# One tile for the split weights, at two offsets: an encoder trunk on one Trainium2 core

## The chip, the core and the metric

The kernel runs on one core of one Trainium2 chip. The metric is the device time of one execution in microseconds; the time of a kernel is the median over its runs. The granted TensorE clock of the profiled execution is 0.999 of full speed.

## What is computed

Two layers of a streaming encoder on 512 tokens of width 1024, all in float32. Cut to what matters here:

```python
def swiglu(x, w_gate, w_up, w_down):
    return (silu(x @ w_gate) * (x @ w_up)) @ w_down        # 1024 -> 2816 -> 1024

for l in range(2):
    x = x + 0.5 * swiglu(rms_norm(x, ffn1_norm[l]), ...)
    h = rms_norm(x, mix_norm[l])
    p = h @ w_in[l]                                        # 1024 -> 1696
    attn = mla_group(...)                                  # latent attention, 8 heads
    conv = conv_group(...)                                 # GLU, causal depthwise conv, LayerNorm
    x = x + concat(attn, conv) @ w_out[l]
    x = x + 0.5 * swiglu(rms_norm(x, ffn2_norm[l]), ...)
    x = rms_norm(x, post_norm[l])
```

The four feed-forward networks (two a layer) hold most of the arithmetic.

## The kernel before

**Products in three parts.** A float32 operand is split into a high part, rounded to the reduced format fp32r that TensorE takes, and a low part, the rest. A product is three matmuls, `mm3` (L171 to L175): high weights with high data (L172), high weights with low data (L173), low weights with high data (L174). In most places the weights are the stationary operand, which a LDWEIGHTS brings into the array ahead of its matmul, and the data are the moving one. Each matmul is 128 by 128 by 256 or 512 columns. In the latent products of the mixer (`latent_k`, `queries`, `keys`, `up_kv`) it is the other way round: data stationary, weights moving.

**Where weights come from.** `load_w` (L149) loads a block of 1024 columns into a tile raw by SyncE's DMA queue, ScalarE casts it to a tile wh (L153), and VectorE (for one kind GpSimd) subtracts to get the tile wl (L159). `half_w` does the same for the first blocks (L1114 to L1118). These are the plain products: the first chunk of each feed-forward network, the down projection of its last chunk, and all of the mixer's products with weights.

**The chunks of the feed-forward network.** `ffn_body` goes through eleven pairs of 256 hidden columns in four chunks. The first chunk of two pairs is computed plainly. The later pairs go through `pair` (L418) with a scheme of seven products in place of eight, on halves of 256 tokens: sums and differences of weight blocks and of activation halves are made by VectorE, and the products are of 256 columns. `product` (L374) takes three matmuls for each; `product_joined` (L385) has high and low data of 256 columns beside each other in one tile xj and needs two: L391 with 512 columns (high weights with both), L392 with 256 (low weights with the high data). Its callers make the weights in two ways. `split_into` (L259) casts a quarter tile fr or raw to wh (L262) and subtracts to wl (L264). `summed` (L411) casts to wh (L415), and its low part is a tile ls, made from the negated copy (L407) to which GpSimd's DMA queue adds the block from memory (L408). `down` (L479) does the same for the down projection of the two middle chunks with 256-column matmuls; its data are ring tiles.

**Where data lie.** Normalized data, products of the gate and most sums are ring tiles r (2048 bytes for each partition, 35 of them). `operands` (L324) makes the sums of the data: those named in `JOINED` and in halves as xj (`joined`, L326), the others in ring tiles (`halved`, L332), and one kind, b22 of the second half, in two tiles xs.

**Where the tiles begin.** Tiles lie in the pools in the order in which their tags first come up. Small tiles `gap0` (16 floats) and `gap1` (32 floats) stand between raw, wh and wl (L1110), and `gap` (`GAP`, L117) stands in the pool of small tiles. Counted modulo 256 bytes with a ring tile as 0, the tiles begin at: wh +64, wl +192; all tiles of the feed-forward pool (fr, xj, xs, ls and others) +96. Every block of 128 columns within a weights tile is 512 bytes, and half a ring tile is 1024, so these offsets hold for every matmul.

**What sets the order.** The tile framework places each engine's instructions by a planned timeline; `tc.issue_after` pins some behind others. A cast waits until the last matmul that reads its slot is done. wh and wl have four slots each.

Of the kernel before, what the change touches and what calls it, by code (L numbers as in the profile page):

```python
# [7 lines left out]
FP = mybir.dt.float32  # L8
FR = mybir.dt.float32r
# [3 lines left out]
ALU = mybir.AluOpType  # L13
AX = mybir.AxisListType

P = 128
D = 1024
S = 512
# [13 lines left out]
NF = F // P  # L32
EPS = 1e-6
WC = 1024
GAP = 96
HS = S // 2
RING = 35
WIDE = 6
# [11 lines left out]
POOLW = "wo"  # L50
# [29 lines left out]
def encoder_kernel(ctx: ExitStack, tc: tile.TileContext, xT, consts, vecs, rgain, wgu1, wd1, wdq1,  # L80
# [6 lines left out]
    wpool = ctx.enter_context(tc.tile_pool(name="w", bufs=4))  # L87
# [4 lines left out]
    def nm(s):  # L92
        uid[0] += 1
        return f"{s}{uid[0]}"
# [21 lines left out]

    small.tile([P, GAP], FP, tag="gap", name="gap", bufs=1)  # L117
    V, A, G, T = nc.vector, nc.scalar, nc.gpsimd, nc.tensor
# [30 lines left out]
    def load_w(src, w, kind=""):  # L149
        raw = wpool.tile([P, WC], FP, tag="raw", name=nm("raw"), bufs=3)  # L150
        nc.sync.dma_start(out=raw[:, :w], in_=src)
        hi = wpool.tile([P, WC], FR, tag="wh", name=nm("wh"))
        order["cast"] = A.copy(hi[:, :w], raw[:, :w]).ins  # L153
        lo = low()
        if kind == "sum":
            A.activation(lo[:, :w], raw[:, :w], AF.Copy, scale=-1.0)
            G.dma_start(out=lo[:, :w], in_=src, accum_op=ALU.add)
            return hi, lo
        (G if kind in POOLW.split() else V).tensor_tensor(lo[:, :w], raw[:, :w], hi[:, :w].bitcast(FP),  # L159
                                                          ALU.subtract)  # L160
        return hi, lo

    def low():
        return wpool.tile([P, WC], FR, tag="wl", name=nm("wl"))

    order = {}

# [82 lines left out]
    def groups(srcs, rhs, ws=None):  # L250

        ws = ws or [load_w(src, WC) for src in srcs]
        os = [bank() for _ in srcs]
        for ks in (range(KD - 1), range(KD - 1, KD)):
            for o, w in zip(os, ws):
                group(o, w, rhs, ks, KD)
        return os

    def split_into(q, src, w=WC):  # L259

        hi = wpool.tile([P, WC], FR, tag="wh", name=nm("wh"))
        A.copy(hi[:, :w], src[:, :w])  # L262
        lo = low()
        order["lo"] = V.tensor_tensor(lo[:, :w], src[:, :w], hi[:, :w].bitcast(FP), ALU.subtract).ins  # L264
        return hi, lo

    def ffn(l, gx, norm, wgu, wd, wdq, gain, done, w0=None, halved=KD):
# [3 lines left out]
    def ffn_body(fpool, l, gx, norm, wgu, wd, wdq, gain, done, w0, halved):  # L271
# [2 lines left out]

        def quarter():
            return fpool.tile([P, WC], FP, tag="fr", name=nm("fr"), bufs=4)
# [124 lines left out]
        def subtracted(w, src, n=WC):  # L404

            lo = fpool.tile([P, WC], FR, tag="ls", name=nm("ls"), bufs=2)
            A.activation(lo[:, :n], src[:, :n], AF.Copy, scale=-1.0)  # L407
            G.dma_start(out=lo[:, :n], in_=w, accum_op=ALU.add)  # L408
            return lo

        def summed(w, src, n=WC, lo=None):  # L411

            lo = subtracted(w, src, n) if lo is None else lo
            hi = wpool.tile([P, WC], FR, tag="wh", name=nm("wh"))
            A.copy(hi[:, :n], src[:, :n])  # L415
            return hi, lo

        def pair(p, quartered):  # L418

            a11, a12, a21, a22, s3 = quarters(wgu[l, p], WC, p == CHUNKS[0][1])  # L420
            bx, by, bz = bank(), (bank(), bank()), (bank(), bank())
            product(bx, split_into("a11", a11), "b11", True, True)
            a = copied(tmp(), bx)
            product_joined(by, summed(wgu[l, p, 1], a12), "b21", True)
# [6 lines left out]
            for c, main, rest in parts(by):  # L431
                V.tensor_tensor(a[:, c], a[:, c], main, ALU.add)
                V.tensor_tensor(a[:, c], a[:, c], rest, ALU.add)
                if c.start == 0:
                    A.activation(s[:, 0:HS], a[:, 0:HS], AF.Silu)
            V.tensor_tensor(s[:, 0:HS], s[:, 0:HS], a[:, HS:S], ALU.mult)
            product(bx, split_into("s2", a11), "t2", False, True)
            r2 = wide(fpool.tile([P, WC], FP, tag="e", name=nm("e"), bufs=1))
            copied(r2[:, 0], bx)
            product_joined(bz, split_into("s3", s3), "t3", True)  # L440
            d = [copied(tmp(), o) for o in bz]
            for t in d:
# [97 lines left out]
        for p0, p1 in CHUNKS:  # L540
# [54 lines left out]
            for m in range(halved if last else KD):  # L595
                if m in ahead:
                    pd, w = ahead[m]
# [440 lines left out]
    class Finish:  # L1038
# [37 lines left out]
        def part(self, h, src, first):  # L1076
            for t in range(2):
                i = T.matmul(self.ss[:, 2 * h + t:2 * h + t + 1], src[:, t * P:(t + 1) * P], ones[:, 0:1],
                             start=first and h == 0 and t == 0, stop=not first, skip_group_check=True)
            return i.ins  # L1080
# [26 lines left out]
    st = Stats()  # L1107
    f = gained(0, "g1", gx, first_gain)
    f(0)
    w0 = [tuple(wpool.tile([P, w], t, tag=tag, name=nm(tag), bufs=n) for t, tag, n, w in (  # L1110
        (FP, "raw", 3, WC), (FP, "gap0", 1, 16), (FR, "wh", 4, WC), (FP, "gap1", 1, 32), (FR, "wl", 4, WC)))[::2]
        for _ in range(2)]

    def half_w(q, gu):  # L1114
        raw, hi, lo = (v[:, gu * 512:(gu + 1) * 512] for v in w0[q])
        nc.sync.dma_start(out=raw, in_=wgu1[0, 0, q, :, gu * 512:(gu + 1) * 512])
        A.copy(hi, raw)  # L1117
        V.tensor_tensor(lo, raw, hi.bitcast(FP), ALU.subtract)  # L1118
    for m in KS:
        if m:  # L1120
            nc.sync.dma_start(out=x[:, m, :], in_=xT[m])
# [6 lines left out]
    w0 = [w[1:] for w in w0]  # L1128
# [172 lines left out]
```

## Time and profile before

| | us |
|---|---|
| median of 3 runs | 1783.02 (1781.78 to 1783.49) |
| the profiled execution | 1781.53 |
| its span, first to last instruction | 1779.8 |
| TensorE, matmuls | 1768.6 busy, 11430 instructions |
| VectorE | 1486.0 busy |
| ScalarE | 1094.9 busy |
| GpSimd | 383.3 busy |

Matmuls are pipelined: the duration of one runs past the start of the next, so busy time and mean duration say little about what a matmul costs. The distance between the starts of neighbouring matmuls does, and the timeline shows it. A group's row has line, engine, operation, output and inputs with buffer numbers left out, shape, count, then busy time, mean duration of one in ns, and the idle time of the engine before it with what ended it.

### The profile page before, as it was taken

What the parts mean: (1) busy time and instruction counts of PE and PEld (TensorE: products, weight loads), DVE (VectorE), ACT (ScalarE), POOL (GpSimd) and SP (SyncE); (2) the same over time, 40 slices, a digit from 0 to 9 for tenths busy, and PEclk for the clock granted to TensorE, in tenths of its full rate; (3) what the DMA queues carried; (4) which work ended last, traced back from release to release, by engine and by line L of the source; (5) the groups of instructions that cost most, each with busy time, mean ns of one, the idle gap of its engine ahead of it and who ended that gap; (6) DMA issues with size and microseconds to landing.
All of it is one profiled execution on the core that took longest, in us unless ns stands there. A gap on an engine that the chain in (4) does not pass through costs nothing.

```text
span 1779.8 us, 29441 instructions
## 1 busy us (share of the span) xinstructions
PE 1768.6 (99%) x11430; PEld 1558.0 (88%) x11430; DVE 1486.0 (83%) x2309; ACT 1094.9 (62%) x1699; POOL 383.3 (22%) x315
## 2 busy tenths in 40 slices
PE   9999999999999999999999999999999999999998
PEld 7899999888678899999888999998976788999997
DVE  7998988588965989998779989876989559999883
ACT  5576766456953575757645757554768435757664
POOL 1000000247822000000310000002576410000002
PEclk9999999999999999999999999999999999999999
DMA  5657574324203466665426575743260125575742
GB/s 170 165 140 186 136 189 114 109 86 124 71 25 101 124 162 162 159 166 131 123 66 167 125 197 124 198 112 112 80 157 24 58 68 155 150 180 140 186 117 74
DMA packets 71947, 228.28 MB, mean 128 GB/s; under 512 B 8448, under 2 KB 9600, under 8 KB 71808
## 3 DMA queue, kind: packets, MB, share of 16 engines
q1 hardware_dynamic: 55536, 171.87, 30.5%
q0 software_dynamic: 16128, 54.53, 18.3%
q8 instruction: 89, 1.46, 0.3%
q14 instruction: 50, 0.41, 0.1%
q10 hardware_dynamic: 144, 0.00, 0.0%
HBM read 222.19 MB, written 2.10 MB: 126 GB/s over the span
## 4 chain that ended last, share of the span: by engine, by line
PE 91%; DVE 5%; ACT 2%; issue 1%; DMA 1%; SPq 0%; ACTq 0%; DVEq 0%
PE ps L172 24%; PE ps L174 24%; PE ps L173 23%; PE ps L391 11%; PE ps L392 6%; DVE cv L972 1%; PE ps L921 1%; DVE mx L880 1%; PE ps L899 1%; DVE wl L264 1%; PE ps L876 0%; PE ps L678 0%; PE ps L216 0%; PE ps L914 0%; DVE r L902 0%
## 5 line engine op out<-in xcount | busy, mean ns | idle before, releaser
L172 PE MATMUL ps<-r,wh 128*128 128x256 f32 (+1 forms) x2556 | 808.8, 320 | 1.7 <-ACT wh L1117 0.6
L173 PE MATMUL ps<-r,wh 128*128 128x256 f32 (+1 forms) x2556 | 807.4, 316 | 0.8 <-DVE r L180 0.4
L174 PE MATMUL ps<-r,wl 128*128 128x256 f32 (+1 forms) x2364 | 753.9, 321 | 0.0
L172 PEld LDWEIGHTS ps<-r,wh 128*128 128x128 f32 x2556 | 480.6, 188 | 51.0 <-issue 3.7
L173 PEld LDWEIGHTS ps<-r,wh 128*128 128x128 f32 x2556 | 480.1, 188 | 42.7 <-DVE r L180 2.5
L174 PEld LDWEIGHTS ps<-r,wl 128*128 128x128 f32 x2364 | 444.1, 188 | 38.5 <-DVE wl L159 0.7
L391 PE MATMUL ps<-xj,wh 128*128 128x512 f32 x864 | 302.5, 390 | 0.0
L153 ACT CAST wh<-raw 128x1024 fp32r<-128x1024 f32 (+3 forms) x148 | 132.4, 900 | 227.9 <-PE ps L173 140.3
L262 ACT CAST wh<-fr 128x1024 fp32r<-128x1024 f32 (+1 forms) x160 | 157.8, 986 | 103.5 <-DVE fr L428 53.2
L159 DVE TENSOR_TENSOR wl<-raw,wh 128x1024 fp32r<-128x1024 f32 (+3 forms) x132 | 142.6, 1089 | 92.5 <-ACT wh L153 91.7
L408 POOL DMA_DIRECT2D ls<-in_wgu x72 | 62.5, 868 | 724.3 <-ACT ls L407 522.5
L264 DVE TENSOR_TENSOR wl<-fr,wh 128x1024 fp32r<-128x1024 f32 (+1 forms) x160 | 182.8, 1143 | 20.2 <-ACT wh L262 20.2
L391 PEld LDWEIGHTS ps<-xj,wh 128*128 128x128 f32 x864 | 160.8, 188 | 29.1
L392 PE MATMUL ps<-xj,ls 128*128 128x256 f32 x576 | 161.3, 280 | 0.0
L978 POOL TENSOR_TENSOR y<-y,pr 128x495 f32<-128x495 f32 (+29 forms) x90 | 120.3, 1339 | 46.6 <-ACT pr L976 41.2
L262 ACT CAST wh<-raw 128x1024 fp32r<-128x1024 f32 (+1 forms) x100 | 97.9, 979 | 42.1 <-PE ps L173 21.1
L264 DVE TENSOR_TENSOR wl<-raw,wh 128x1024 fp32r<-128x1024 f32 (+1 forms) x100 | 113.8, 1138 | 11.8 <-ACT wh L262 11.2
L392 PEld LDWEIGHTS ps<-xj,ls 128*128 128x128 f32 x576 | 108.1, 188 | 0.0
L209 POOL TENSOR_TENSOR r<-r,t 128x512 f32<-128x512 f32 x45 | 75.3, 1681 | 133.3 <-ACT t L205 132.7
L407 ACT ACTIVATE ls<-fr 128x1024 fp32r<-128x1024 f32 (+1 forms) x56 | 56.1, 1001 | 73.3 <-PE ps L392 41.5
L972 DVE SCALAR_TENSOR_TENSOR cv<-m,vec,cv 128x511 f32<-128x511 f32 (+14 forms) x120 | 88.1, 734 | 4.6 <-ACT cv L968 3.0
L408 POOL DMA_DIRECT2D ls<-in_wdq x32 | 27.6, 863 | 258.6 <-ACT ls L407 258.6
(258 smaller groups left out, 2921.5 us busy)
## 6 DMA issues: line engine op xcount, KB each, us to landing
fr<-in_wgu SPq DMA_DIRECT2D x112, 512.0 KB, 4.2
ls<-in_wgu POOLq DMA_DIRECT2D x72, 512.0 KB, 6.6
raw<-in_wgu SPq DMA_DIRECT2D x62, 512.0 KB, 4.6
fr<-in_wdq SPq DMA_DIRECT2D x48, 384.0 KB, 4.7
ls<-in_wdq POOLq DMA_DIRECT2D x32, 384.0 KB, 4.9
raw<-in_wd SPq DMA_DIRECT2D x32, 384.0 KB, 3.2
raw<-in_wd SPq DMA_DIRECT2D x32, 256.0 KB, 2.8
raw<-in_wcv SPq DMA_DIRECT2D x16, 512.0 KB, 3.6
```

Of the source, the lines that this page charges most:

```text
L153: order["cast"] = A.copy(hi[:, :w], raw[:, :w]).ins
L159: (G if kind in POOLW.split() else V).tensor_tensor(lo[:, :w], raw[:, :w], hi[:, :w].bitcast(FP), ALU.subtract)
L172: T.matmul(o, lh, rh, start=first, stop=False, skip_group_check=free)
L173: T.matmul(o, lh, rl, start=False, stop=False, skip_group_check=free)
L174: order["mm"] = T.matmul(o, ll, rh, start=False, stop=last, skip_group_check=free).ins
L262: A.copy(hi[:, :w], src[:, :w])
L264: order["lo"] = V.tensor_tensor(lo[:, :w], src[:, :w], hi[:, :w].bitcast(FP), ALU.subtract).ins
L391: T.matmul(o, w[0][:, c], both, start=start and k == 0, stop=False, skip_group_check=True)
L392: last = T.matmul(o[:, 0:HS], w[1][:, c], both[:, 0:HS], start=False, stop=k == 3, skip_group_check=True).ins
L408: G.dma_start(out=lo[:, :n], in_=w, accum_op=ALU.add)
L972: V.scalar_tensor_tensor(acc[:, s:], u[c][:, :S - s], tap(k), acc[:, s:], ALU.mult, ALU.add)
L978: order["conv"] = G.tensor_tensor(ys[c][:, s:], ys[c][:, s:], pr[:, s:], ALU.add).ins
```

## The change

Three things are changed.

*One weights tile.* wh, wl, gap0 and gap1 are gone. A tile `weights` of 2 x 4 x 1024 floats and 48 more holds four slots for the high parts and then four for the low ones. `part(j, moved)` hands out the next slot of the high (0) or low (1) parts. For `load_w` and `half_w` a slot begins at 0 from a ring tile (modulo 256 bytes); for `split_into` and `summed` (`moved`) it begins 16 floats further for a high part and 48 for a low one: +64 and +192, as before. A moved slot reaches into the first bytes of the slot behind it; where the kind changes from moved to plain, one slot is skipped.

*Order.* `in_turn` pins the high casts behind each other in the order of the program, and the low subtractions of each engine too.

*The pool of the feed-forward network.* Its tags are brought up at the start in another order, xj, xs, a gap of 48 floats, ls, and then the rest, and `GAP` is 72. So xj and xs begin at 0 from a ring tile, ls and fr at +192.

The diff, cut to its core:

```diff
-GAP = 96
+GAP = 72
+WN = 4
+WOFF = 16, 48
@@ load_w
-        hi = wpool.tile([P, WC], FR, tag="wh", name=nm("wh"))
-        order["cast"] = A.copy(hi[:, :w], raw[:, :w]).ins
+        hi = part(0)
+        order["cast"] = in_turn("h", lambda: A.copy(hi[:, :w], raw[:, :w]))
         lo = low()
...
-        (G if kind in POOLW.split() else V).tensor_tensor(lo[:, :w], raw[:, :w], hi[:, :w].bitcast(FP),
-                                                          ALU.subtract)
+        e = G if kind in POOLW.split() else V
+        in_turn(e, lambda: e.tensor_tensor(lo[:, :w], raw[:, :w], hi[:, :w].bitcast(FP), ALU.subtract))
         return hi, lo

-    def low():
-        return wpool.tile([P, WC], FR, tag="wl", name=nm("wl"))
+    weights = wpool.tile([P, 2 * WN * WC + WOFF[1]], FR, name="weights", bufs=1)
+    used, was = [0, 0], [False, False]
+
+    def part(j, moved=False):
+        if was[j] and not moved:
+            used[j] += 1
+        was[j] = moved
+        i = (j * WN + used[j] % WN) * WC + (WOFF[j] if moved else 0)
+        used[j] += 1
+        return weights[:, i:i + WC]
+
+    turns = {}
+
+    def in_turn(key, make):
+        with tc.issue_after(turns[key]) if key in turns else nullcontext():
+            turns[key] = make().ins
+        return turns[key]
+
+    def low(moved=False):
+        return part(1, moved)
@@ split_into (summed likewise for its high part)
-        hi = wpool.tile([P, WC], FR, tag="wh", name=nm("wh"))
-        A.copy(hi[:, :w], src[:, :w])
-        lo = low()
-        order["lo"] = V.tensor_tensor(lo[:, :w], src[:, :w], hi[:, :w].bitcast(FP), ALU.subtract).ins
+        hi = part(0, True)
+        in_turn("h", lambda: A.copy(hi[:, :w], src[:, :w]))
+        lo = low(True)
+        order["lo"] = in_turn(V, lambda: V.tensor_tensor(lo[:, :w], src[:, :w], hi[:, :w].bitcast(FP), ALU.subtract))
@@ ffn_body, at its start
+        fpool.tile([P, 2, S], FR, tag="xj", name=nm("xj"), bufs=WIDE)
+        fpool.tile([P, S], FR, tag="xs", name=nm("xs"), bufs=2)
+        fpool.tile([P, 48], FP, tag="gap", name=nm("gap"), bufs=1)
+        fpool.tile([P, WC], FR, tag="ls", name=nm("ls"), bufs=2)
@@ the first blocks
-    w0 = [tuple(wpool.tile([P, w], t, tag=tag, name=nm(tag), bufs=n) for t, tag, n, w in (
-        (FP, "raw", 3, WC), (FP, "gap0", 1, 16), (FR, "wh", 4, WC), (FP, "gap1", 1, 32), (FR, "wl", 4, WC)))[::2]
-        for _ in range(2)]
+    w0 = [(wpool.tile([P, WC], FP, tag="raw", name=nm("raw"), bufs=3), part(0), part(1)) for _ in range(2)]
@@ half_w
-        A.copy(hi, raw)
-        V.tensor_tensor(lo, raw, hi.bitcast(FP), ALU.subtract)
+        in_turn("h", lambda: A.copy(hi, raw))
+        in_turn(V, lambda: V.tensor_tensor(lo, raw, hi.bitcast(FP), ALU.subtract))
```

The order on the engines stays nearly the same; the largest moves are six places on ScalarE and one stretch of 24 matmuls passing 24 others on TensorE. Line numbers of the changed kernel are larger: L153 becomes L155, L262 becomes L284, L401 becomes L428, L313 becomes L340, L179 becomes L201, L328 and L336 become L355 and L363. Two places on ScalarE follow. The first is at the start of the first down projection (the casts of 512 columns to wh are those of its weights). Before:

```order
L241 COPY r_341<-ps_339 128x512
L313 ACTIVATE t_387<-t_385 128x512
L328 CAST xj_417<-fr_408 128x2x256
L336 CAST xs_704<-fr_520 128x512
L313 ACTIVATE t_398<-t_396 128x512
L153 CAST wh_536<-raw_534 128x512
L153 CAST wh_552<-raw_550 128x512
L179 CAST r_392<-t_389 128x512
```

Now:

```order
L263 COPY r_330<-ps_328 128x512
L155 CAST weights<-raw_519 128x512
L340 ACTIVATE t_376<-t_374 128x512
L155 CAST weights<-raw_533 128x512
L355 CAST xj_406<-fr_397 128x2x256
L363 CAST xs_675<-fr_505 128x512
L340 ACTIVATE t_387<-t_385 128x512
L201 CAST r_381<-t_378 128x512
```

The two casts of weights stand ahead of the joined operand xj and of the tile xs, where they stood behind them.

The second is the end of the last pair, where the weights of the last chunk (768 columns) begin. Before:

```order
L435 ACTIVATE t_3424<-t_3397 128x256
L401 COPY t_3481<-ps_3367 128x512
L153 CAST wh_3587<-raw_3585 128x768
L401 COPY t_3483<-ps_3368 128x512
L153 CAST wh_3619<-raw_3617 128x768
L401 COPY e_3459<-ps_3364 128x512
L153 CAST wh_3652<-raw_3650 128x768
```

Now:

```order
L462 ACTIVATE t_3246<-t_3220 128x256
L428 COPY t_3299<-ps_3192 128x512
L428 COPY t_3301<-ps_3193 128x512
L155 CAST weights<-raw_3398 128x768
L428 COPY e_3279<-ps_3189 128x512
L155 CAST weights<-raw_3428 128x768
L481 ACTIVATE t_3358<-e_3279 128x512
L155 CAST weights<-raw_3459 128x768
```

Each cast of the last chunk's weights stands one copy or activation later.

More of the change, by code (lines that the diff above doesn't have):

```diff
@@ L413, in summed @@
             lo = subtracted(w, src, n) if lo is None else lo
-            hi = wpool.tile([P, WC], FR, tag="wh", name=nm("wh"))
-            A.copy(hi[:, :n], src[:, :n])
+            hi = part(0, True)
+            in_turn("h", lambda: A.copy(hi[:, :n], src[:, :n]))
             return hi, lo
```

## The prediction

> **What bounds the kernel now.** I read the page first, then the groups of instructions with shapes kept apart, then TensorE's waits, then its timeline in five quiet stretches. From the page:
>
> ```profile
> span 1779.8 us, 29441 instructions
> ...
> PE 1768.6 (99%) x11430; PEld 1558.0 (88%) x11430; DVE 1486.0 (83%) x2309; ACT 1094.9 (62%) x1699; POOL 383.3 (22%) x315
> ...
> PEclk9999999999999999999999999999999999999999
> ...
> PE 91%; DVE 5%; ACT 2%; issue 1%; DMA 1%; SPq 0%; ACTq 0%; DVEq 0%
> ```
>
> TensorE is busy all the time, at full clock, and holds 91% of the chain that ended last. Its waits, all of them:
>
> ```profile
> engine line waited for: us in total, times, longest us
> PE ps L133 <- DVE ones L129: 1.1, 1, 1.1
> PE ps L876 <- ACT r L884: 1.0, 2, 0.5
> PE ps L172 <- ACT wh L1117: 0.6, 1, 0.6
> PE ps L173 <- DVE r L180: 0.4, 1, 0.4
> ```
>
> So nothing that feeds TensorE is worth much; the time is the number of matmuls times the distance from one start to the next. The counts that matter, by line and shape:
>
> ```profile
> L172 PE MATMUL ps<-r,wh 128*128 128x256 f32 x1704 | 477.4, 280 | 1.0
> L172 PE MATMUL ps<-r,wh 128*128 128x512 f32 x852 | 331.3, 399 | 0.7 <-ACT wh L1117 0.6
> L391 PE MATMUL ps<-xj,wh 128*128 128x512 f32 x864 | 302.5, 390 | 0.0
> L392 PE MATMUL ps<-xj,ls 128*128 128x256 f32 x576 | 161.3, 280 | 0.0
> L392 PE MATMUL ps<-xj,wl 128*128 128x256 f32 x288 | 78.1, 281 | 0.0
> L174 PE MATMUL ps<-r,ls 128*128 128x256 f32 x192 | 54.3, 283 | 0.0
> L172 PE MATMUL ps<-xs,wh 128*128 128x256 f32 x144 | 40.4, 280 | 0.0
> L172 PE MATMUL ps<-m,wh 128*128 128x512 f32 x16 | 6.5, 406 | 0.0
> ```
>
> The mean durations there overlap each other, so they are no price; a price is the distance between starts. The timeline of TensorE gives it: two rows each, the first and the last of a run. Columns are start, duration, engine and line.
>
> ```profile
> 100.50 0.28 PE L172 MATMUL ps<-r,wh 128*128 128x256 f32 x1
> ...
> 102.20 0.28 PE L172 MATMUL ps<-r,wh 128*128 128x256 f32 x1
> ```
>
> 15 matmuls of 256 columns from ring tiles in 1.70 us: **113 ns**. The same shape and lines from the tiles xs:
>
> ```profile
> 92.40 0.28 PE L172 MATMUL ps<-xs,wh 128*128 128x256 f32 x1
> ...
> 93.11 0.28 PE L172 MATMUL ps<-r,wh 128*128 128x256 f32 x1
> ```
>
> 6 in 0.71 us: **118 ns**. And from ring tiles, but with low weights in ls:
>
> ```profile
> 135.83 0.28 PE L174 MATMUL ps<-r,ls 128*128 128x256 f32 x1
> ...
> 136.90 0.29 PE L174 MATMUL ps<-r,ls 128*128 128x256 f32 x1
> ```
>
> 9 in 1.07 us: **119 ns**, all three matmuls of the group, though two of them read the same kinds of tile as the 113 ns ones. The joined products, first with ls, then with wl:
>
> ```profile
> 305.04 0.39 PE L391 MATMUL ps<-xj,wh 128*128 128x512 f32 x1
> ...
> 307.80 0.40 PE L172 MATMUL ps<-r,wh 128*128 128x512 f32 x1
> ```
>
> ```profile
> 299.85 0.39 PE L391 MATMUL ps<-xj,wh 128*128 128x512 f32 x1
> ...
> 302.28 0.28 PE L172 MATMUL ps<-r,wh 128*128 128x256 f32 x1
> ```
>
> 8 pairs in 2.76 us, **345 ns** a pair; 7 pairs in 2.43 us, **347 ns**. Last a stretch of nothing but plain products of 512 columns, as the view by stages has it:
>
> ```profile
> 516.00:556.00 40.00, 40.00 (x174) 1.00 0.34 105
> ```
>
> 173 distances in 40 us: **231 ns**. What differs between the 113 and the 118 ns is where the operands begin. Modulo 256 bytes, with a ring tile as zero, before the change: wh +64, wl +192, and everything in the FFN's pool (xj, xs, ls) +96. So the pair of 113 ns is ring data with weights at +64 and +192; each run with something at +96 is 5 to 6 ns slower per matmul.
>
> **The change, part by part.** It removes no operation and adds none; it moves operands.
>
> *xs.* xs goes to 0, its weights stay at +64 and +192: offset for offset the 113 ns case. 3 x 144 = 432 matmuls x 5 ns = **-2.2 us**. Bounds: 0 if xs is slow for another reason, -2.6 at the 6 ns that ls shows.
>
> *ring tiles with ls.* ls goes to +192, where wl is: again the 113 ns case. 3 x 192 = 576 x 5.6 ns = **-3.2 us**; bounds 0 and -3.5.
>
> *Joined products.* xj goes to 0, its low weights, ls or wl, to +192, its high ones stay at +64. No run of before has this with 512 columns in alternation with 256. The 256-wide half should fall from 118 to 113 as above. The 512-wide half is 345 - 118 = 227 ns now with ls, which lies on xj's own offset, and 229 with wl; with the weights apart as in the plain stage it may cost 231. A pair is 340 to 349 ns, by 113 + 227 and 118 + 231. I take 344, since the one half gains about what the other loses: 576 x 1 + 288 x 3 = **-1.4 us**; bounds -4.9 and +2.9.
>
> *Plain products of 512 columns.* This is the large term and the open one. Weights that come in through load_w now begin at the ring tiles' own offset, high and low. 852 + 16 groups of three, 2604 matmuls, at 231 ns now. The only run of before in which the stationary operand loaded next has the offset of the moving one is the joined product with ls, and that is the cheapest of its width, 227 ns against 229 with wl and 231 here. I take 227: 2604 x 4.5 ns, since the stage's distance is 231.2 and a half of 226.7 goes to it, = **-11.7 us**. The bounds are the best and the worst rate per column of the 256-wide runs: twice 113.3 is 226.6, -12 us; twice 118.3 is 236.6, +14 us. The value taken lies next to the good end because the nearest row in kind, the same width at the same relative offset, lies there; the bad end stays in the range.
>
> The Trainium skill speaks against any term here: "SBUF — State Buffer", section "Who interferes with whom", gives TensorE two independent read ports, one for the moving operand and one for the weights, and says that it never waits on anyone. By that rule all terms would be zero. The trace has 113 and 118 ns for one shape and one pair of lines, so the rule does not tell the whole.
>
> *Latent products.* Here the weights are the moving operand and ring tiles the stationary one:
>
> ```profile
> L172 PE MATMUL ps<-wh,r 128*128 128x288 f32 x64 | 18.9, 295 | 0.0
> L172 PE MATMUL ps<-wh,r 128*128 128x384 f32 x48 | 16.6, 347 | 0.0
> L172 PE MATMUL ps<-wh,r 128*128 128x512 f32 x32 | 12.7, 398 | 0.0
> ```
>
> They go from +64 and +192 to 0 as well. 3 x 144 = 432 matmuls; at the 2% of the plain term either way this is 1.5 us or so. I take -0.5.
>
> *Casts in program order, and slots.* The order shows casts of load_w moved by a few places on ACT, and all else in place. Where the kernel goes from moved weights to plain ones, one slot of four is skipped, so the first casts of the last chunk wait for later matmuls than before, 12 to 20 of them, 2 to 4 us.
>
> ```profile
> 302.36 0.83 ACT L153 CAST wh<-raw 128x768 fp32r<-128x768 f32 x1 [0.44 <-PE ps L391]
> ```
>
> This first one ends at 303.19 and is first used at 307.80 (the row above), 4.6 us later; that slack hides the wait. On ACT the copies L401 and then L454 stand behind it, and TensorE waits for their banks. If the cover were gone it would cost up to 1 us at each of the four ends of an FFN. I take 0, bounds -1 and +4. The casts brought forward at the first down projection wait on ACT for fresh weights, with the joined operands' casts behind them, which are not due for several us.
>
> Sum: -2.2 - 3.2 - 1.4 - 11.7 - 0.5 = **-19.0 us**. The profiled execution took 1781.5 us (span 1779.8 and 1.7 around it), the median of the runs is 1783.0; 1781.5 - 19.0 = 1762.5, and against the median **1764 us**.
>
> **Rivals.**
> - *Plain products don't care.* If only +96 is bad, and 0, +64 and +192 are alike, the plain and latent terms vanish: -6.8, **1776 us**. For it: 113 ns holds for +64 and +192 alike. Against it: 512-wide products are dearer per column there (231 for 512, 113 for 256) than the joined one at equal offset.
> - *Equal offsets collide* (the other side). Weights and moving data start being read together, at the same place in the 256 bytes, in each of 2604 plain matmuls, and each takes 236.6: +14 for these, +1.5 for the latent ones, -6.8 for the rest, **1792 us**. It decides from about 234 ns a matmul, where its loss eats the 6.8 us. For it: nothing in the trace repeats equal offsets matmul after matmul, so the one row I lean on may owe its 227 ns to the other shape between. Against it: the 227 ns.
> - *Offsets are not the cause.* xs and ls are slow by their place in the sequence, not their address; nothing changes, **1783 us**. For it: two of the three matmuls in the ls groups read ordinary tiles and are slow too. Against it: xs and ring tiles alternate in the timeline around 92 us, in the same loop, and the distance follows the tile. The rule of the Trainium skill named above ("SBUF — State Buffer") gives this too.
> - *Slots.* One tile with overlapping offsets makes casts late at each change of kind, with TensorE waiting: 8 changes x 1 us, and more if the waits cover whole tiles: -19 + 25, about **1789 us**. Against it: the slack of 4.6 us.
>
> **How the numbers follow.** My forecast 50%; plain products indifferent 17%; collision 22%; not the offsets 6%; slots 5%. A measurement of this kernel tells about 0.2%, 3.6 us. Faster by more: the first two and a mild collision (below 234 ns), 0.68. Within: the third and what lies at the edge, 0.07. Slower: collision and slots, 0.25. The forecast's own range is 1757 to 1772. For 8 in 10 the range takes in the indifferent case at 1776 and part of the collision: 1755 to 1788.
>
> **What would show it.** After, in the same views: xs and the ls groups at 113 ns a matmul; joined pairs at 344; a plain stage of 40 us with 176 distances, not 173 (227 ns) if I am right, 169 (236.6) if they collide; TensorE's waits as short as now. I am wrong if the plain stage keeps 231 or rises, or if ACT or DVE appear in its waits with more than 4 us.

## The result, and the profile after

The changed kernel takes **1773.99 us** (median of 5 runs, 1773.26 to 1775.6), the kernel before in the same comparison 1782.10 (1781.78 to 1783.49). The ratio is 0.9953, with an interval of 0.9939 to 0.9966: faster by 8.1 us, where 19.0 were forecast. The profiled execution of after took 1775.60 us, the highest of its five, and its span is 5.9 us shorter than that of before. From the page of after, the span, the engines, and the chain of work that ended last:

```profile
span 1773.8 us, 29449 instructions
...
PE 1757.2 (99%) x11430; PEld 1555.0 (88%) x11430; DVE 1488.6 (84%) x2309; ACT 1095.9 (62%) x1699; POOL 381.3 (21%) x315
...
PE 33%; DVE 3%; ACT 1%; issue 0%; DMA 0%; ACTq 0%; DVEq 0%
```

TensorE is still busy all the time. The chain holds 37% of the span in all, so in this execution it was not followed to the start, and its shares say nothing beside the 91% of before. TensorE's waits, in the view that had four rows and 3.1 us before (line waited at, engine and line waited for; total, times, longest):

```profile
PE ps L196 <- DVE weights L162: 2.3, 3, 0.9
PE ps L903 <- ACT r L911: 1.5, 3, 0.5
PE ps L194 <- ACT weights L1142: 1.4, 1, 1.4
PE ps L195 <- DVE r L202: 1.3, 8, 0.2
PE ps L135 <- DVE ones L131: 1.1, 1, 1.1
PE ps L196 <- DVE weights L286: 0.8, 3, 0.3
PE ps L194 <- ACT weights L155: 0.4, 1, 0.4
PE ps L884 <- DVE r L929: 0.4, 1, 0.4
```

Eight rows and 9.2 us. New at the top is a wait for VectorE's low subtraction of the weights, L162 (L159 before), and casts of weights (L155) stand there too. VectorE's rows come to 5.9 us (1.5 before), over the 4 us that the prediction named as a sign that it is wrong. TensorE's rate, first by stages: the quiet stretch of plain products that held 174 matmuls before.

```profile
516.00:556.00 40.00, 40.00 (x178) 1.00 0.34 105
```

Now 178, so 177 distances in 40 us, 226 ns each. In the timeline (start, duration, engine, line), the first and the last row of four runs; L194, L195 and L196 are the three lines of `mm3`, L418 and L419 those of the joined product. Products with xs, then ring tiles with low weights in ls, then joined ones (with a row two pairs into the run), then the ring tiles behind these:

```profile
93.57 0.28 PE L194 MATMUL ps<-xs,weights 128*128 128x256 f32 x1
...
94.25 0.28 PE L194 MATMUL ps<-r,weights 128*128 128x256 f32 x1
...
136.92 0.28 PE L196 MATMUL ps<-r,ls 128*128 128x256 f32 x1
...
137.94 0.28 PE L196 MATMUL ps<-r,ls 128*128 128x256 f32 x1
...
301.05 0.39 PE L418 MATMUL ps<-xj,weights 128*128 128x512 f32 x1
...
301.74 0.40 PE L418 MATMUL ps<-xj,weights 128*128 128x512 f32 x1
...
303.86 0.28 PE L194 MATMUL ps<-r,weights 128*128 128x256 f32 x1
...
304.57 0.28 PE L194 MATMUL ps<-r,weights 128*128 128x256 f32 x1
```

xs: 6 in 0.68 us, **113 ns**; ls: 9 in 1.02 us, **113 ns**; both as forecast. Joined: the first two pairs of a run of eight in 0.69 us, 345 ns each, but the other six in 2.12 us, **353 ns** each. And the six ring matmuls that follow take 118 ns and not 113.

All start-to-start distances of TensorE, added up over the two traces by kind of product. A distance more than 30 ns above the usual one of its shape (113 ns for 256 columns, 227 for 512) is a gap, and only the excess is counted there:

| | before, us | after, us | difference | forecast |
|---|---|---|---|---|
| plain, 512 columns | 603.5 | 591.3 | -12.2 | -11.7 |
| ring tiles, 256 columns, with ls among them | 588.6 | 584.7 | -3.9 | -3.2 |
| xs | 51.3 | 49.1 | -2.2 | -2.2 |
| latent | 72.8 | 72.4 | -0.4 | -0.5 |
| joined | 298.9 | 302.7 | **+3.8** | -1.4 |
| gaps | 19.8 | 27.7 | **+7.9** | 0 |
| the rest | | | +1.1 | 0 |
| sum | | | -5.9 | -19.0 |

Four terms are right to within 0.7 us. Of the 13 us that are missing, 5.2 are in the joined products and 7.9 in gaps. The gaps by place:

| gaps, us | before | after |
|---|---|---|
| first 35 us of the program | 1.6 | 2.4 |
| ends of the four first chunks (within 15 us of 60, 605, 945, 1483 us) | 0.9 | 4.4 |
| the pairs behind these (before the change: to 313, 855, 1195 and 1737 us) | 11.9 | 15.5 |
| elsewhere | 5.4 | 5.4 |

The part at the start is not the same in every execution: over the runs below that leave the start as it is, it lies between 1.6 and 2.4 us.

### The profile page after: what moved, and what is told of

It is laid out like the page before. It is cut to its first block, busy times and chain, and to the rows that moved or that the text cites. A ratio compares the mean times of both kernels' runs of the same rounds, so it can differ in the third digit from the quotient of the medians.

```text
span 1773.8 us, 29449 instructions
## 1 busy us (share of the span) xinstructions
PE 1757.2 (99%) x11430; PEld 1555.0 (88%) x11430; DVE 1488.6 (84%) x2309; ACT 1095.9 (62%) x1699; POOL 381.3 (21%) x315
## 5 line engine op out<-in xcount | busy, mean ns | idle before, releaser
L194 PE MATMUL ps<-r,weights 128*128 128x256 f32 (+1 forms) x2556 | 804.6, 318 | 2.8 <-ACT weights L1142 1.4
L195 PE MATMUL ps<-r,weights 128*128 128x256 f32 (+1 forms) x2556 | 804.4, 315 | 1.3 <-DVE r L202 1.3
L196 PE MATMUL ps<-r,weights 128*128 128x256 f32 (+1 forms) x2364 | 750.2, 319 | 3.2 <-DVE weights L162 2.3
L194 PEld LDWEIGHTS ps<-r,weights 128*128 128x128 f32 x2556 | 480.0, 188 | 50.2 <-ACT t L428 4.5
L195 PEld LDWEIGHTS ps<-r,weights 128*128 128x128 f32 x2556 | 480.6, 188 | 37.7 <-DVE r L202 2.8
L196 PEld LDWEIGHTS ps<-r,weights 128*128 128x128 f32 x2364 | 444.0, 188 | 39.4 <-DVE weights L162 3.6
L418 PE MATMUL ps<-xj,weights 128*128 128x512 f32 x864 | 306.4, 395 | 0.0
L155 ACT CAST weights<-raw 128x1024 fp32r<-128x1024 f32 (+3 forms) x148 | 131.7, 902 | 213.6 <-PE ps L195 120.7
L284 ACT CAST weights<-fr 128x1024 fp32r<-128x1024 f32 (+1 forms) x160 | 157.3, 983 | 100.3 <-DVE fr L455 51.8
L435 POOL DMA_DIRECT2D ls<-in_wgu x72 | 62.7, 871 | 724.9 <-ACT ls L434 664.3
L162 DVE TENSOR_TENSOR weights<-raw,weights 128x1024 fp32r<-128x1024 f32 (+3 forms) x132 | 142.8, 1090 | 81.0 <-ACT weights L155 79.9
L286 DVE TENSOR_TENSOR weights<-fr,weights 128x1024 fp32r<-128x1024 f32 (+1 forms) x160 | 182.3, 1139 | 21.3 <-ACT weights L284 21.3
L418 PEld LDWEIGHTS ps<-xj,weights 128*128 128x128 f32 x864 | 161.5, 188 | 31.0
L419 PE MATMUL ps<-xj,ls 128*128 128x256 f32 x576 | 162.5, 282 | 0.0
L284 ACT CAST weights<-raw 128x1024 fp32r<-128x1024 f32 (+1 forms) x100 | 97.8, 978 | 43.9 <-PE ps L195 22.9
L286 DVE TENSOR_TENSOR weights<-raw,weights 128x1024 fp32r<-128x1024 f32 (+1 forms) x100 | 113.5, 1135 | 11.4 <-ACT weights L284 10.9
L419 PEld LDWEIGHTS ps<-xj,ls 128*128 128x128 f32 x576 | 108.6, 189 | 0.0
L435 POOL DMA_DIRECT2D ls<-in_wdq x32 | 27.7, 865 | 258.2 <-ACT ls L434 258.2
```

The costliest lines, as they stand in the source:

```text
L155: order["cast"] = in_turn("h", lambda: A.copy(hi[:, :w], raw[:, :w]))
L162: in_turn(e, lambda: e.tensor_tensor(lo[:, :w], raw[:, :w], hi[:, :w].bitcast(FP), ALU.subtract))
L194: T.matmul(o, lh, rh, start=first, stop=False, skip_group_check=free)
L195: T.matmul(o, lh, rl, start=False, stop=False, skip_group_check=free)
L196: order["mm"] = T.matmul(o, ll, rh, start=False, stop=last, skip_group_check=free).ins
L284: in_turn("h", lambda: A.copy(hi[:, :w], src[:, :w]))
```

## The experiments

Twelve kernels were run. Where nothing else is said, the edit is made to the changed kernel; ratios are to the kernel before.

### Which edit makes the joined products dear

**The pool alone.** The kernel before, with only the third of the three changes; the weights stay in tiles of their own at +64 and +192.

```diff
-GAP = 96
+GAP = 72
+        fpool.tile([P, 2, S], FR, tag="xj", name=nm("xj"), bufs=WIDE)
+        fpool.tile([P, S], FR, tag="xs", name=nm("xs"), bufs=2)
+        fpool.tile([P, 48], FP, tag="gap", name=nm("gap"), bufs=1)
+        fpool.tile([P, WC], FR, tag="ls", name=nm("ls"), bufs=2)
```

> The kernel before with only the feed-forward pool rearranged: xj and xs at 0 from a ring tile, ls at +192; weights as before. Theory (what counts is the offset between a matmul's moving data and the weights that are loaded while it runs): xs and ring-with-ls groups 113 ns a matmul, joined pairs 353 ns as in the changed kernel, plain products 231 ns, TensorE's long gaps 20 us in all as before; -2.2 -3.7 +5 = about 1781 us. Rival (the joined products became dearer because of the shared weights tile or the new order): pairs stay at 345 ns and the time is 1776 us.

Measured: 1783.0 us, ratio 0.9999 (0.999 to 1.0009). In its timeline, a run of eight joined pairs with ls:

```profile
305.46 0.39 PE L396 MATMUL ps<-xj,wh 128*128 128x512 f32 x1
...
306.15 0.40 PE L396 MATMUL ps<-xj,wh 128*128 128x512 f32 x1
...
308.27 0.40 PE L172 MATMUL ps<-r,wh 128*128 128x512 f32 x1
```

345 ns a pair for the first two, 353 for the other six, as in the changed kernel; all joined distances without gaps are 302.8 us (298.9 before). Plain products stay at 231 ns (603.6 us in all), xs and ls are at 113. So the new places in this pool make the joined products dear, without the single tile and without the pins; the next four kernels part xj from ls. The 3.9 us that this costs and 4.0 us more of gaps (23.8 against 19.8, nearly all outside the ends of the first chunks) eat what xs and ls gain: the third change alone is worth nothing.

**xj elsewhere.** Four kernels put xj at another offset and leave everything else where it is. The edit for +96; for +64 and +128 the two gaps are 16 and 32, and 32 and 16 floats, and for +192 xj comes behind the gap of 48 floats:

```diff
-        fpool.tile([P, 2, S], FR, tag="xj", name=nm("xj"), bufs=WIDE)
         fpool.tile([P, S], FR, tag="xs", name=nm("xs"), bufs=2)
-        fpool.tile([P, 48], FP, tag="gap", name=nm("gap"), bufs=1)
+        fpool.tile([P, 24], FP, tag="gapa", name=nm("gapa"), bufs=1)
+        fpool.tile([P, 2, S], FR, tag="xj", name=nm("xj"), bufs=WIDE)
+        fpool.tile([P, 24], FP, tag="gapb", name=nm("gapb"), bufs=1)
```

At +192:

> The changed kernel with xj at +192, where its low weights (ls and wl) begin; its high weights are then 128 away. Theory: the 512-wide joined matmul, which runs while the low weights are loaded, has equal offsets and falls from 233 to 227 ns; the 256-wide one is open at a distance of 128, 113 to 120: a pair 340 to 347 ns, 864 x 6 to 13 = 5 to 11 us less, 1763 to 1769 us. Rival (it is the alternation of two widths that costs, not the offset): pairs stay at 353, 1774 us.

At +96:

> The changed kernel with xj back at +96, where it lay before; xs, ls and the weights stay where the change put them. Theory (the pair's cost is set by where xj lies against its high and low weights, and by nothing else of the change): pairs 347 ns, as they were before with wl at +192; 864 x 6 ns = 5 us less, 1769 us. Rival (the shared weights tile or the speed around it): pairs stay at 353, 1774 us.

At +128:

> As the last, with xj at +128: its low weights are then 64 on, its high ones 64 back. If a joined matmul likes what the 256-wide ring products like (weights 64 away on either side), pairs come to 340 to 345 ns; if only +96 was good, to 350 or more.

At +64:

> As the last, with xj at +64: high weights at equal offset, low ones 128 away. The 256-wide matmul runs while high weights are loaded and took 120 ns at equal offsets in the changed kernel's few plain 256-wide products; so a 256-wide half of 120 and a pair of 350 or more. If equal offsets suit the joined matmul whichever weights they are, a pair under 347.

Measured (high weights at +64, low ones at +192 in all of them; the median over 864 pairs, and medians by their place in a run of eight):

| xj at | pair, ns | first to eighth pair of a run | joined without gaps, us | span, us | median, us |
|---|---|---|---|---|---|
| 0 (the change) | 353 | 344 346 353 353 353 353 353 354 | 302.7 | 1773.8 | 1773.99 |
| +64 | 347 | 348 349 346 347 346 347 346 348 | 300.0 | 1769.9 | 1771.64 (one run) |
| +96 | 347 | 348 347 346 347 346 347 346 347 | 299.9 | 1771.5 | 1773.44 |
| +128 | 346 | 343 344 346 347 346 347 346 348 | 299.3 | 1769.5 | 1771.48 (one run) |
| +192 | 352 | 349 352 358 352 347 351 352 359 | 304.7 | 1774.7 | 1775.16 |

Three things follow. The offset 0 costs 2.7 to 3.4 us of joined distances against 64 to 128, and as nothing else moves, it is the place of xj that does it. The equal offset of the weights loaded next, on which the 227 ns of the forecast rested, does not explain the joined product: at +192 the low weights lie on xj's own offset, and the pair is 352, not the 340 to 347 that this theory gave; and at +64 the high weights lie on it, and the pair is 347, not the 350 or more that was expected. And the price at 0 is not one number: it is 344 at the head of a run, what the forecast took, and 353 from the third pair on.

The cheaper pairs are not all gained. TensorE's weight loads wait for an eviction on ScalarE at 24 of the 108 ends of joined runs. The first row is from the changed kernel, the second from the one with xj at +128:

```profile
PEld ps L194 <- ACT t L428: 4.5, 24, 0.2
PEld ps L194 <- ACT t L429: 5.8, 24, 0.2
```

In the kernel before, this row has 0.3 us and 2 waits. The distance from the joined product to the next group is 113 to 117 ns at these 24 places there, 146 to 153 in the change, and about 205 with xj at +64 to +128. With these gaps included, the joined distances are 303.6 us at 0 and 302.2, 302.2 and 301.4 us at +64, +96 and +128, so a half to two thirds of the difference is left. Why the eviction ends later than it did before, no run shows.

**Runs of one width.** Two kernels take the eight matmuls of a joined product in another order, four of 512 columns and then four of 256.

```diff
-                    for k in range(4):
-                        both = X[n][k // 2][:, k % 2]
+                    for j in range(2):
+                        for k in range(4):
+                            both = X[n][k // 2][:, k % 2]
...
+                            if j == 0:
                                 T.matmul(o, w[0][:, c], both, ...)
+                            else:
                                 last = T.matmul(o[:, 0:HS], w[1][:, c], both[:, 0:HS], ...)
```

With xj at 0, as in the change:

> The changed kernel with xj where it puts it, at 0 (high weights at +64, low ones at +192), and with the matmuls of a joined product in the order four of 512 columns, four of 256. Nothing is left out. Theory: in runs of one width the two halves cost what ring tiles with the same weights cost in runs: 231 ns for 512 columns and 113 for 256, so 344 a pair in place of 353, 864 x 9 ns = 8 us less than the changed kernel: 1766 us. This would say that the step that failed in the forecast, a pair as the sum of halves taken from runs of one width, fails by the alternation alone. Rival: the tile xj at 0 is dear in any order (its half with 256 columns stayed at 119 or 120): a pair at 350 to 353 and the time of the changed kernel.

With xj at +64:

> The changed kernel with xj at +64, so that its high weights lie on its own offset and its low ones 128 bytes away, and with the eight matmuls of a joined product in another order: first the four of 512 columns, then the four of 256, where so far the two kinds alternated. Nothing is left out. With the old order this placing had 347 ns a pair (230 + 117). If the alternation of widths is what makes the halves cost otherwise than in runs of one width, the 512-wide ones come to the 227 ns of the plain stage, which has the same relative offset, the 256-wide ones to 113 to 120, and a pair to 340 to 347: with 864 pairs 0 to 6 us less than with the old order, so a span of 1764 to 1770 us. If a half costs what its two tiles make it cost, in whatever order, a pair stays at 347 and the span near 1770.

Measured with xj at 0: 1771.49 us, ratio 0.9932 (0.9918 to 0.9947). A joined stretch of its timeline, where matmuls that overlap without a break are one row with their count:

```profile
299.95 1.08 PE L420 MATMUL ps<-xj,weights 128*128 128x512 f32 x4
300.87 0.63 PE L422 MATMUL ps<-xj,weights 128*128 128x256 f32 x4
301.34 1.09 PE L420 MATMUL ps<-xj,weights 128*128 128x512 f32 x4
302.26 0.63 PE L422 MATMUL ps<-xj,weights 128*128 128x256 f32 x4
302.74 0.28 PE L194 MATMUL ps<-r,weights 128*128 128x256 f32 x1
...
303.07 0.28 PE L194 MATMUL ps<-r,weights 128*128 128x256 f32 x1
```

Eight of 512 and eight of 256 in 2.79 us, 349 ns a pair; over the trace the medians inside the runs are 231 and 118 ns. The 512-wide half costs what the theory said, the 256-wide one does not come down to 113. And the ring group behind the run takes 0.33 us at once; with the alternating order the first two groups behind a joined run take 356 and 357 ns and only the fourth is at 340 (medians over 72 to 108 places). That is where this kernel gains: with gaps the joined distances are 303.4 us, against 303.6 in the changed kernel, but the ring tiles of 256 columns take 582.0 us and not 584.7. With xj at +64: 1773.77 us, ratio 0.9945 (0.993 to 0.996), 231 ns for the 512-wide ones, though their weights lie on xj's own offset, which gives 227 with ring tiles, and 122 for the 256-wide ones; 305.4 us of joined distances, gaps included, in place of the 302.2 of the alternating order there. The theory that runs are cheaper fell there. What both runs show is that the relative offset of the two operands of a matmul does not fix its price: 512 columns at equal offsets take 227 ns from ring tiles and 231 from xj.

### What the plain products are worth

The weights of the plain products go back to +64 and +192, in the new single tile, with the pins, and with no slot skipped.

```diff
-        hi = part(0)
+        hi = part(0, True)
...
-        lo = low()
+        lo = low(True)
...
-        ... part(0), part(1)) for _ in range(2)]
+        ... part(0, True), part(1, True)) for _ in range(2)]
```

> The changed kernel with the plain weights at +64 and +192 too, so that no kind of weights has the ring tiles' offset and no slot is skipped. Theory: the plain matmuls go back from 227 to 231 ns, 2604 x 4.7 ns = +12 us, 1786 us, the joined pairs stay at 353. If the skipped and overlapping slots caused the longer gaps, these fall from 28 to 20 us and the time is 1778 us; if the order pins did, they stay at 28. Rival (the plain gain came from the order): plain stays at 227.

Measured: 1784.61 us, ratio 1.0007 (0.9997 to 1.0016). Its plain stage is back at the count of before:

```profile
516.00:556.00 40.00, 40.00 (x174) 1.00 0.32 96
```

The plain distances are 603.5 us, as before the change, and 591.3 with it. So the offset of the plain weights is worth 10.6 us between the medians (1784.61 - 1773.99) and carries the whole gain: without it the change is no faster than the kernel before. Joined pairs stay at 353. The gaps are 26.8 us, 2.5 of them at the ends of the first chunks, so most of them do not come from skipped slots.

### Where the gaps come from

At the end of the first chunk TensorE takes the down projection's weights, which ScalarE casts and VectorE subtracts. ScalarE there, before the change:

```profile
61.54 1.06 ACT L407 ACTIVATE ls<-fr 128x1024 fp32r<-128x1024 f32 x1 [1.07 <-DMA fr<-in_wgu]
62.51 0.60 ACT L153 CAST wh<-raw 128x512 fp32r<-128x512 f32 x1
63.01 0.61 ACT L328 CAST xj<-t 128x512 fp32r<-128x512 f32 x1
```

and after:

```profile
62.10 0.60 ACT L363 CAST r<-t 128x512 fp32r<-128x512 f32 x1
62.61 0.62 ACT L355 CAST xj<-t 128x512 fp32r<-128x512 f32 x1
63.13 1.66 ACT L155 CAST weights<-raw 128x512 fp32r<-128x512 f32 x3
```

VectorE before, and then after:

```profile
62.73 1.89 DVE L607 SCALAR_TENSOR_TENSOR x<-ps,x 128x512 f32<-128x512 f32 x3
64.53 0.69 DVE L159 TENSOR_TENSOR wl<-raw,wh 128x512 fp32r<-128x512 f32 x1
```

```profile
63.94 0.68 DVE L356 TENSOR_TENSOR xj<-t,xj 128x512 fp32r<-128x512 f32 x1
64.54 1.28 DVE L634 SCALAR_TENSOR_TENSOR x<-ps,x 128x512 f32<-128x512 f32 x2
65.74 0.68 DVE L162 TENSOR_TENSOR weights<-raw,weights 128x512 fp32r<-128x512 f32 x1
```

And TensorE after, at the same place:

```profile
65.18 0.39 PE L195 MATMUL ps<-r,weights 128*128 128x512 f32 x1
66.48 0.50 PE L196 MATMUL ps<-r,weights 128*128 128x512 f32 x1 [0.90 <-DVE weights L162]
```

The casts of this projection's weights now stand behind two casts of operand sums for the first pair (L363, L355), and the subtraction starts at 65.74 us, not 64.53, behind the low part of such a sum (L356) and two evictions. TensorE stands from one matmul to the next for 1.30 us in place of 0.23. Four experiments ask why.

**Without the pins** of casts and subtractions:

```diff
-        with tc.issue_after(turns[key]) if key in turns else nullcontext():
-            turns[key] = make().ins
+        turns[key] = make().ins
```

> The changed kernel without the pins that keep casts in program order. Theory A (the pins cause the 8 us of longer gaps): gaps back to 20 us, 1766 us. Theory B (TensorE runs ahead of feeders that have not become faster, so the gaps are what it gains and gives back): gaps stay near 28 us, 1774 us. All distances without gaps as in the changed kernel.

Measured: 1787.69 us, ratio 1.0027 (1.0017 to 1.0037). Gaps 38.9 us. The top of TensorE's waits:

```profile
PE ps L194 <- DVE r L201: 4.1, 8, 0.8
PE ps L195 <- DVE weights L285: 3.6, 9, 1.2
PE ps L195 <- DVE weights L162: 2.4, 3, 0.9
```

The gaps at the ends of the first chunks are 4.2 us, about the 4.4 with the pins. The pins do not make these gaps; with one tile they save 13.7 us (1787.69 - 1773.99 between the medians).

**The low subtractions of that projection on GpSimd** in place of VectorE:

```diff
-                    ahead[m] = bank(), load_w(..., fn * P)
+                    ahead[m] = bank(), load_w(..., fn * P, "wo")
...
-                    group(pd, load_w(..., fn * P), act, range(fn), fn)
+                    group(pd, load_w(..., fn * P, "" if p0 else "wo"), act, range(fn), fn)
```

> The changed kernel with the low parts of the first chunk's down weights subtracted on GpSimd, 32 subtractions of 0.69 us taken from VectorE. Theory A (TensorE now reaches the end of the first chunk before VectorE has worked off its sums, so the plain gain is given back there): the gaps at the four ends of the first chunk fall from 4.4 us to under 1.5, 1771 us. Theory B (the casts on ScalarE or the slots are late, not VectorE): gaps there stay at 4 us or grow, 1774 us or more.

Measured: 1775.63 us, ratio 0.996 (0.9945 to 0.9975); gaps at the ends of the first chunks 5.4 us, more than the 4.4. The wait has moved:

```profile
PE ps L195 <- DVE r L202: 2.2, 9, 0.9
PE ps L903 <- ACT r L911: 1.5, 3, 0.5
PE ps L194 <- ACT weights L155: 1.1, 3, 0.4
```

TensorE no longer waits for L162 but for the data's low parts (L202, VectorE) and for the casts of the weights (ScalarE). That VectorE is late with these subtractions alone is not the cause.

**The sums later.** The sums for the first pair are no longer made between the steps of this projection, but at its end.

```diff
                 if p0 == 0:
-                    advance(2)
+                    advance(0)
```

In this kernel the operands from the second half of x's rows are made after the projection has already been added to x, so from other values than in the changed kernel; the number and the shapes of the instructions are the same.

> The changed kernel, with the sums of data for the first pair no longer advanced between the steps of the first chunk's down projection but all at its end; nothing is left out. On VectorE no joined operand then stands between the low subtractions of that projection. Theory: TensorE's gaps at the ends of the four first chunks (4.4 us of the changed kernel against 0.9 before) come from those sums, which stand ahead of the down projection's casts and subtractions on ScalarE and VectorE; then these gaps fall below 1.5 us there, and what the sums cost shows up where the first pair begins, if it cannot be hidden: between -3 us and +5 us in all. Rival: the gaps come from the weights' own way (load, cast and slot), whatever stands beside it; then they stay at 4 to 5 us. The joined pairs stay at 353 ns and the plain matmuls at 227 in both cases.

Measured: 1827.68 us, ratio 1.0253 (1.0236 to 1.027). Within the down projections of the four first chunks, which lie up to 39 us later here, **no gap** is left (4.4 us in the changed kernel, under 1.5 by the theory). The price appears where the first pair begins, and is far over the 5 us of the expectation:

```profile
PE ps L194 <- ACT weights L284: 27.0, 4, 7.2
PE ps L419 <- DMA ls<-in_wgu: 9.5, 4, 3.4
PE ps L196 <- DVE weights L286: 4.9, 6, 1.7
```

Four waits, one for each feed-forward network, of up to 7.2 us for the first pair's weights. Not all of the price is waiting: behind these waits the granted clock fell (0.50 from 643 to 648 us, 0.987 over the execution, 1.0 in the changed kernel), and 12.5 of the 81.2 us of gaps are matmuls at up to twice their usual distance.

**The sums earlier**, with xj at +128: twelve steps of them between the plain products of the first chunk and so fewer in the projection.

```diff
-                        advance(8)
+                        advance(12)
```

> The changed kernel with xj 128 bytes further, where a joined pair had 346 ns, and with the sums of data for the first pair made earlier: twelve steps of them between the plain products of the first chunk in place of eight, so that fewer are left for the down projection behind it. Nothing is left out. Theory: as the gaps at the ends of the first chunks come from these sums, which stand ahead of the down projection's casts and low subtractions, they fall from the 4.1 us that xj 128 bytes further had with eight steps to 1 to 3 us, and the time from 1771.5 to 1769 or 1770. Rival: the sums only change places with other work of the same engines, the gaps stay at 4 us or move into the plain products of the first chunk, and the time is 1771 to 1774. The pairs stay at 346 and the plain matmuls at 227 in both.

Measured: 1782.71 us, ratio 1.0 (0.9991 to 1.0009). The gaps at these ends do not fall but rise, to 14.0 us; neither theory had that. TensorE's first row of waits, and then ScalarE at one of the four places:

```profile
PE ps L194 <- ACT r L201: 8.7, 4, 3.0
```

```profile
61.28 1.06 ACT L435 ACTIVATE ls<-fr 128x1024 fp32r<-128x1024 f32 x1 [4.59 <-DMA fr<-in_wgu]
62.25 0.60 ACT L356 CAST xj<-t 128x512 fp32r<-128x512 f32 x1
62.75 0.61 ACT L201 CAST r<-t 128x512 fp32r<-128x512 f32 x1
```

ScalarE stands 4.59 us at the head of its queue for a block of the first pair's weights (L435), with the cast that TensorE waits for (L201, the high part of the projection's own data) two places behind it. The planner had put it there once the sums were earlier. At two of the four places the granted clock fell behind the wait:

```profile
604.00:608.00 4.00, 4.00 (x12) 0.59 0.91 188
```

The 0.59 is the mean granted clock of this window; matmuls of 512 columns stand 427 ns apart where it is low, and 3.2 of the 14.0 us come from this and not from waiting. So the work for the first pair on ScalarE and VectorE does set these gaps: without the sums there none, as they are 4.4, otherwise placed 14.0. But earlier is not better.

## Why the prediction was right and wrong

**What bounds the kernel**: right. TensorE stays 99% busy, and the change acts through the distance between starts.

**xs and ls**: right, in size and place, 113 ns each, in the pool experiment alone too.

**Plain products**: the size is right (-12.2 us for -11.7), and the experiment on them shows that their offset is what does it. The Trainium skill ("SBUF — State Buffer", section "Who interferes with whom") has TensorE's two reads independent and waiting for nobody. The traces do not bear that out: putting the plain weights back by 64 and 192 bytes changes the plain distances by 12.2 us. The reason given for the 227 ns, a likeness to the joined product with equal offset, is not shown. At +192 and in runs of one width with xj at +64, equal offset did not give the joined product the low price; 227 at equal offset holds for ring tiles. So the size came out right for a reason that did not hold elsewhere, which is in part luck.

**Latent products**: right, -0.4 us.

**Joined products**: this step failed. It took a pair as the sum of a 256-wide half at 113 ns, from runs of ring tiles, and a 512-wide half between 227 and 231, and put 344. The forecast bounds, -4.9 and +2.9, rested on the same addition, and +3.8 is outside them. The runs showed in its place: 344 only for the first pair of a run, 353 from the third on; and 118 and not 113 for the 256-wide half even in runs of its own with these offsets. The groups behind a run are dear too, but so they were before (357, 356 and then 340 ns). A price read from the steady part of one sequence was carried to another sequence, where it does not hold.

**Casts in order, and slots**: this step failed too, with 0 us taken, +4 as its upper bound and +7.9 measured. It looked at the casts that were moved ahead, found sums behind them that are "not due for several us", and put the risk at the first casts of the last chunk. The gaps at the ends of the first chunks grew in the other direction: later casts and subtractions of the same projection stand behind the sums. They are 1.0 us with the pool alone, 2.5 with one tile and pins at the old plain rate, and 4.4 at the new one. The last step, 1.9 us, comes with the faster plain products: TensorE reaches the place sooner and what feeds it does not, so part of the gain is given back. That is argued from these three kernels and not shown: the kernel at the old plain rate also skips no slot, and no run changed the feeding alone by so much. Of the other 4.5 us of gaps (7.9 less 3.4), 3.7 lie in the pairs, and the pool alone has most of them there too (15.1 us, 11.9 before and 15.5 with the change); 0.8 of these are the 24 waits for an eviction. Some 0.7 lie in the first 35 us, which vary from run to run. The profiled execution is 1.6 us over the median of its kernel, but six kernels that move only xj or reorder the joined matmuls have 25.8 to 28.5 us of gaps in all, so the growth from 19.8 is not chance. What makes the rest of the gaps in the pairs stays open.

**Rivals.** The time is within 2 us of the rival in which plain products do not care (1776), and that rival is wrong: they fell by 12.2 us, and two other terms came out 13 us worse than forecast. Colliding equal offsets did not come for 512 columns. For 256 columns they did: 21 groups of plain products of that width went from 340 to 360 ns, 0.4 us in all. That the offsets are not the cause is refuted by the experiment on the plain weights. Waits at each change of kind of slot were not what was seen: the kernel that skips no slot has 26.8 us of gaps too.

**The combined versions.** xj at +64 and +128 gave 1771.64 and 1771.48 us in one run each, and xj at 0 in runs of one width 1771.49 (interval of the ratio to 0.9947, that of the changed kernel from 0.9939: they overlap). So some 2.5 us more are likely to be had from the joined products and the groups behind them, though the intervals do not yet part them from the changed kernel.

## What to carry to other kernels

When TensorE is busy to the end, compare the start-to-start distance of equal shapes before anything else; where it differs by tile, where the operands begin may be the reason, and one edit that moves only one operand settles it. Do not add up a price for a new sequence from the steady distances of others: read the head, the steady part and what follows of a run apart, and try two or three offsets. And when the engine that bounds the kernel gets faster at one place, ask of each feeder there what stands ahead of it in its queue that is due later.

## What the runs showed that was not expected

The distance between matmuls has a memory. With xj at 0 the first two pairs of a run cost 344 and 346 ns and all others 353 (medians over 108 runs); the ring groups behind a joined run cost 356, 357, 343 and then 340 (medians over 72 to 108 places), though all have the same tiles and offsets; and with the joined matmuls in runs of one width the group behind is at 341 at once with xj at 0, and at 355 and then 340 with xj at +64. What one matmul leaves for the next in this way no run shows.
